# A two-layer trunk on one core: the delta rule's triangular system from raw keys without 48 transposes, weight buffers in memory of their own, last transposes pinned to later matmuls

## Chip, core and metric

The kernel runs on one NeuronCore of a Trainium2 chip. Its time is device microseconds of one execution, from start to end on that core. Time before: 2292.58 us, the median of three runs.

## What is computed

Two layers over 256 tokens with 2048 features, all in float32. Layer 0 mixes the tokens by eight heads of differential attention and eight heads of a gated delta rule. Layer 1 mixes them by sixteen heads of attention in three dilations. Behind each mixer stands an MLP with 8192 hidden features and a squared ReLU. The change touches the delta rule, which the reference states in chunks:

```python
bq = l2_norm(bq); bk = l2_norm(bk)              # keys and queries to length 1
g = -exp(b_a_log) * softplus(ba + b_dt_bias);   beta = sigmoid(bb)
q = q * dk ** -0.5;   gc = cumsum(g)
decay_incl = exp(where(causal, gc[:, None] - gc[None, :], -inf))
kb = k * beta[..., None]
m = (kb @ k.T) * strict(decay_incl)
rhs = concat([v * beta[..., None], kb * exp(gc)[..., None]])
u, w = triangular_solve(eye + m, rhs)           # unit lower triangular
attn = (q @ k.T) * decay_incl
# step over chunks: v_new = u - w @ state;  o = (q*exp(gc)) @ state + attn @ v_new
#                   state = state * exp(g_last) + (k*exp(g_last - gc)).T @ v_new
```

and the frame around it:

```python
x = x + diff_delta_mixer(rms_norm(x, ab_norm), ...)   # w_in 2048 x 7184, w_out 2048 x 2048
x = x + squared_relu_mlp(rms_norm(x, mlp_norm[0]), mlp_w1[0], mlp_w2[0])
x = x + dilated_mixer(rms_norm(x, c_norm), ...)       # w_in 2048 x 6144, w_out 2048 x 2048
x = x + squared_relu_mlp(rms_norm(x, mlp_norm[1]), mlp_w1[1], mlp_w2[1])
```

## The kernel before

**Dense products.** Every product with a weight matrix goes through `dense` (L191). A weight tile of 128 features by 512 columns is loaded by the SP queue (`wload`, L176), split into a high part by a cast on ScalarE (ACT, tile names ending in `h`, L204) and a low part by a subtraction on VectorE (DVE, ending in `l`, L205, recorded at the helper's line L107). Each half of the 256 tokens then takes three matmuls on TensorE (PE): high by high (L210), high by low (L211), low by high (L212). The split weights lie in `wq[0]`, a memory pool of six slots of each part. Casts and subtractions are put 60 places ahead in the order (`high_priority(offset=AHEAD)`).

**Order of the work.** The program is written out flat, and a scheduler fixes each engine's order at compile time from program order, priorities and its own estimate of when inputs are ready. Everything between the dense products is written as generators in three streams, `g` (delta rule), `s` (convolutions, attention, norms) and `o` (outputs). `drip()` in `dense` advances `g` and `s` in turn, one step for each 128 features, so that a step of `g` comes once in two. `flush` advances them all without dense work between. `issue_after(ins)` makes the instructions that are traced inside it come after `ins` on the same engine.

**Layer 0's mixer** (0 to about 450 us, then the output products `wo` to 510.7 us). `do_b` computes q and k of two heads, `do_bv` v, `do_a` and `do_av` the differential attention's, and the gates come with `z2`. `gdn` (L617) works on one pair of heads `s` at a time, four pairs one behind the other (tiles `g0` to `g3`), each with two heads and two chunks of 128 tokens, that is four 128 x 128 tiles. In its steps: `qk` is turned to token-major by transposes on PE (`kp`, `qp`), squared and summed, and the keys `kh` are scaled to length 1. The row `dd` of cumulated gates is read back from DRAM by a DMA and made the decay. `kh` is transposed back (`kt` into `khT`), `pk` is key times key, `m` is `pk` by beta and decay. `m` goes to DRAM and its 16 x 16 diagonal blocks come back (`mb`) to be inverted on DVE; `m` is also transposed (`tt` into `mT`). `pa` is query times key, `am` is that by the decay, and it is transposed as well (second `tt` into `aT`). Then two levels of block elimination (`lp`, `ly`, `lx`), `u` and `w`, the state, and the output.

**Small operations.** `tt`, `stt` and `ts` are DVE's (L107, L113, L117 or L119), `act` is ACT's (L123, L125), `transpose` is PE's (L235). PSUM tiles of the small matmuls come from two pools of two buffers each, `ps_t` for transposes and `ps_m` for products.

**Transitions.** `next_norm` (L295) prepares the next stage's left operand from a finished quarter `n` of `x` (512 features): sums of squares, then transposes to feature-major (`xb`, `xc`, `xd`), split like the weights. The last quarter (`n == 3`) is transposed on PE in the first dense product of the next stage. The stages open memory pools one after the other; what one stage frees, the next takes. Before, `wq0` is the first pool of the first mixer and `wq1`, `wq2` and `wq3` take the same place in the next stages.

Of the kernel before, what the change touches and what calls it, by code (L numbers as in the profile page):

```python
# [19 lines left out]
P = 128  # L20
# [30 lines left out]
def _constants():  # L51
# [36 lines left out]
def trunk(  # L88
# [145 lines left out]
    def transpose(o, i, k=P):  # L234
        E.transpose(o, i, ident[:k, :k])  # L235
# [51 lines left out]
    def turn_quadrant(src, dst, i):  # L287
# [3 lines left out]
        for j in range(4):  # L291
            dv = dst[32 * j:32 * j + 32].rearrange("p c (h t) -> p h c t", h=NH)
            V.transpose(out=dv[:, :, :, q], in_=sv[:, :, :, j, :])  # L293

    def next_norm(n, norm, nm, dst, pool=None):  # L295

        stats_block(xs[n], n, nm + "s")
        if n == 3:
            for _ in range(3):
                yield  # L300
        yield from xt_block(xs[n], n, norm, nm, dst, pool if n < 3 else None)
        if n == 3:
            stats_end(nm + "e")
            yield

    def add_to_x(n, ps):
# [49 lines left out]

    sp.tile([P, 96], F32, tag="fill", name="fill", bufs=1)
    warm = sp.tile([P, 512], F32, tag="junk", name="warm")
# [19 lines left out]
    with ExitStack() as mix:  # L378
        wq[0] = mix.enter_context(tc.tile_pool(name="wq0", bufs=1))
        op = mix.enter_context(tc.tile_pool(name="op", bufs=1))  # L380
# [19 lines left out]
        def behind(gen):  # L400

            while True:
                with tc.issue_after(last_mm[0].ins):
                    if next(gen, gen) is gen:
                        return
                yield

# [93 lines left out]
        beta = mp.tile([P, NH, 8], F32, name="beta")  # L501
        nbeta = mp.tile([P, NH, 8], F32, name="nbeta")
        gg = mp.tile([P, NH, 8], F32, name="gg")
# [7 lines left out]
        def gates(a, b):  # L511
            ts(beta, b, 0.5, 0.5, ALU.mult, ALU.add)
            ts(nbeta, beta, -1.0, None, ALU.mult)
            tt(a, a, dtb.unsqueeze(1).broadcast_to([P, NH, 8]), ALU.add)
# [29 lines left out]
            act(flat(egl), e, AF.Exp)  # L544
            ngc = sp.tile([P, 16], F32, tag="ngc", name="ngc")
            ts(ngc, flat(gc), -1.0, None, ALU.mult)
            yield
            pc = ps_t("pgt")
            transpose(pc[:16, :P], ngc)
            row = sp.tile([P, 512], F32, tag="junk", name="grow_t")[:16, :P]  # L550
# [47 lines left out]
        def v_side(raw, rnm, g, vb, nm):  # L598
            a = mp.tile([P, 4, T], F32, tag="qka", name=nm + "a")
            yield from conv(raw, rnm, [16 + 4 * g + c for c in range(4)], a, nm)  # L600
            for h in range(NH):
                t = ps_t(f"{nm}v{h}")
                for c in range(4):
                    transpose(t[:, c * P:(c + 1) * P], a[:, c, h * P:(h + 1) * P])
                tt(vb[:, h], quads(t), beta[:, h, 4 * g:4 * g + 4].unsqueeze(2).broadcast_to([P, 4, P]), ALU.mult)
            ready.add(f"v{g}")
            yield

        def qk_conv(raw, rnm, s, qks):
# [5 lines left out]
            ready.add(f"qk{s}")  # L615

        def gdn(qks, s, vb, nm):  # L617

# [8 lines left out]
            kh = mt("kh")  # L627
            for w, o, c in (("k", 0, 2), ("q", 4, 0)):
# [6 lines left out]
                if w == "k":  # L635
                    S.copy(kh, quads(pt))
            yield
            rs = mp.tile([P, 8], F32, tag="g_rs", name=nm + "rs")
            rsqrt(rs, ssq, 8, 1.0, nm)
            for i in range(4):  # L640
                ts(kh[:, i, :], kh[:, i, :], rs[:, i:i + 1], None, ALU.mult)
            sq = mp.tile([P, 4], F32, tag="g_sq", name=nm + "sq")
            ts(sq, rs[:, 4:8], 128.0 ** -0.5, None, ALU.mult)

            dd = mt("dd")
            nc.sync.dma_start(
                dd.rearrange("p (h e) c -> p h e c", h=NH),
                bass.AP(scg.tensor, scg.offset + 2 * s * P, [[0, P], [8 * P, NH], [P, 2], [1, P]]))
            for i, (h, e) in enumerate(tiles):
                hd = 2 * s + e  # L650
                stt(dd[:, i, :], dd[:, i, :], gc[:, h, hd:hd + 1], cst("causal"), ALU.add, ALU.min)
            act(dd, dd, AF.Exp)
            for _ in range(3):
                yield
            khT, kd, kbg = mt("khT"), mt("kd", n=2), mt("kbg", n=2)
# [3 lines left out]
            S.copy(khT, quads(t))  # L659
            for e in range(2):  # L660
                hd = 2 * s + e
                ts(kd[:, e, :], kh[:, e, :], egl[:, 0, hd:hd + 1], None, ALU.mult)
                ts(kbg[:, e, :], kh[:, 2 + e, :], egc[:, 1, hd:hd + 1], beta[:, 1, hd:hd + 1], ALU.mult, ALU.mult)
            yield
            m, am = mt("m"), mt("am")
            pk = ps_m(nm + "pk")
            for i, (h, e) in enumerate(tiles):
                E.matmul(pk[:, i * P:(i + 1) * P], lhsT=khT[:, i, :], rhs=khT[:, i, :], start=True, stop=True)
            for i, (h, e) in enumerate(tiles):
                hd = 2 * s + e  # L670
                stt(m[:, i, :], pk[:, i * P:(i + 1) * P], nbeta[:, h, hd:hd + 1], dd[:, i, :], ALU.mult, ALU.mult)

            scr, sxy = scm[s % 2], scx[s % 2]
            nc.sync.dma_start(images(scr), m)
# [3 lines left out]
            mT, aT = mt("mT"), mt("aT")  # L678
# [16 lines left out]
            for j in range(3):  # L695
                n, w = 3 - j, j + 1
                tv = tm[:, :4 * n * w].rearrange("p (b r c) -> p b r c", b=4, r=n)
                xr = part(x0, (j + 1) * BLK, B4, (BLK, n), (1, w))
                tt(tv, part(mb, (j + 1) * BLK + j, B4, (BLK, n), (0, w)), part(x0, j * BLK, B4, (0, n), (1, w)), ALU.mult)
                tt(xr, tv, xr, ALU.add)  # L700
            for b in (4, 8):
                for d in range(0, BLK, 2 * b):
# [3 lines left out]
                    full = [32, b, b, b]  # L706
                    tt(tv, mb[:, lo, hi].unsqueeze(2).broadcast_to(full),
                       x0[:, hi, hi].rearrange("p k c -> p c k").unsqueeze(1).broadcast_to(full), ALU.mult)
# [14 lines left out]
            yield  # L723
            pa = ps_m(nm + "pa")
            for i, (h, e) in enumerate(tiles):
                E.matmul(pa[:, i * P:(i + 1) * P], lhsT=qk[:, e, h * P:(h + 1) * P], rhs=khT[:, i, :], start=True, stop=True)
# [4 lines left out]
            for i in range(4):  # L731
# [31 lines left out]
            while f"v{s // 2}" not in ready:  # L763
                yield
            yield
            u, wT = mt("u", share="m"), mt("wT", n=2, share="khT")
# [435 lines left out]
```

## Time and profile before

| | |
|---|---|
| median of three runs | 2292.58 us (2292.51 to 2294.17) |
| the profiled execution | 2293.58 us; span from first to last instruction 2291.8 us |
| mean granted TensorE clock | 0.999 |
| PE busy | 2279.2 us, 99% of the span, 10536 matmuls |
| PE weight loads | 1887.6 us, 82% |
| DVE busy | 1670.6 us, 73% |
| ACT busy | 1195.0 us, 52% |
| DMA | 420.11 MB read, 185 GB/s over the span |
| first mixer | 0 to 510.7 us |
| first MLP | to 1209.3 us |
| second mixer | to 1589.3 us |
| second MLP | to 2291.8 us |

Matmuls are pipelined, and their recorded durations overlap: a 512-column matmul is recorded with 0.39 us and the next starts 0.23 us after it. What a piece of work costs PE is therefore read from starts, not from durations. A float32 matmul of the small products stands as two records, a transpose as one. An engine's idle time is put down to what released it.

### The profile page before, as it was taken

To read this page: it belongs to the slowest core of one execution; us is meant where nothing else is said; L and a number is where in the kernel's file an instruction comes from. 1 tells how busy PE (TensorE), PEld (TensorE's weight loads), DVE (VectorE), ACT (ScalarE), POOL (GpSimd) and SP (SyncE) were. 2 spreads that over 40 slices of the span, in tenths; PEclk is the share of its full clock that TensorE was granted. 3 is DMA by queue.
4 is the path that set the end of the run, shared out by engine and by line. 5 is a ranking of instruction groups with operands and counts; after the bars stand their busy time and mean duration, and the time that the engine had idled before them with its cause. 6 is when DMAs were issued, how large, how long until landed. Compare 5 with 4: busy or idle time off the path is not lost.

```text
span 2291.8 us, 29876 instructions
## 1 busy us (share of the span) xinstructions
PE 2279.2 (99%) x10536; PEld 1887.6 (82%) x10536; DVE 1670.6 (73%) x3027; ACT 1195.0 (52%) x1865; POOL 5.6 (0%) x15
## 2 busy tenths in 40 slices
PE   9999999999999999999999999999999999999999
PEld 8887888788888888888888888888888888888887
DVE  6868797867757746846888888986775775775774
ACT  6557666655534534534545565555543543543553
POOL 0000000000000000000000000000000000000000
PEclk9999999999999999999999999999999999999999
DMA  8655564456666666666656555555666666666665
GB/s 259 192 172 159 143 182 134 141 177 199 200 194 186 200 194 189 197 195 190 194 192 193 183 176 176 174 184 168 194 194 194 194 194 194 191 195 194 188 208 165
DMA packets 271546, 426.54 MB, mean 186 GB/s; under 512 B 22386, under 2 KB 102436, under 8 KB 271396
## 3 DMA queue, kind: packets, MB, share of 16 engines
q1 hardware_dynamic: 271220, 424.57, 61.3%
q8 instruction: 82, 1.34, 0.3%
q14 instruction: 68, 0.56, 0.1%
q10 hardware_dynamic: 176, 0.07, 0.0%
HBM read 420.11 MB, written 4.46 MB: 185 GB/s over the span
## 4 chain that ended last, share of the span: by engine, by line
PE 94%; DVE 3%; DMA 1%; ACT 1%; issue 1%; SPq 0%; ACTq 0%
PE m_0p L211 3%; PE n_2p L211 3%; PE n_1p L212 3%; PE n_0p L212 3%; PE m_3p L212 3%; PE m_3p L210 3%; PE m_2p L212 3%; PE m_2p L210 3%; PE m_1p L212 3%; PE m_1p L210 3%; PE n_0p L210 3%; PE n_1p L211 3%; PE n_2p L212 3%; PE m_0p L212 3%; PE n_2p L210 3%; PE n_1p L210 3%
## 5 line engine op out<-in xcount | busy, mean ns | idle before, releaser
L107 DVE TENSOR_TENSOR n_3l<-n_3r,n_3h 128x1024 fp32r<-128x1024 f32 x64 | 78.4, 1224 | 76.8 <-ACT n_3h L204 76.7
L107 DVE TENSOR_TENSOR n_2l<-n_2r,n_2h 128x1024 fp32r<-128x1024 f32 x64 | 78.4, 1224 | 76.8 <-ACT n_2h L204 76.7
L107 DVE TENSOR_TENSOR m_0l<-m_0r,m_0h 128x1024 fp32r<-128x1024 f32 x64 | 78.1, 1225 | 73.4 <-ACT m_0h L204 73.0
L107 DVE TENSOR_TENSOR n_1l<-n_1r,n_1h 128x1024 fp32r<-128x1024 f32 x64 | 78.4, 1224 | 67.7 <-ACT n_1h L204 66.9
L204 ACT CAST n_2h<-n_2r 128x1024 fp32r<-128x1024 f32 x64 | 67.5, 1054 | 100.2 <-PE n_2p L212 59.9
L204 ACT CAST n_3h<-n_3r 128x1024 fp32r<-128x1024 f32 x64 | 67.5, 1054 | 100.2 <-PE n_3p L212 59.9
L204 ACT CAST m_0h<-m_0r 128x1024 fp32r<-128x1024 f32 x64 | 67.1, 1054 | 97.2 <-PE m_0p L212 59.9
L204 ACT CAST n_1h<-n_1r 128x1024 fp32r<-128x1024 f32 x64 | 67.5, 1054 | 92.8 <-PE n_1p L212 59.9
L107 DVE TENSOR_TENSOR m_1l<-m_1r,m_1h 128x1024 fp32r<-128x1024 f32 x64 | 78.4, 1225 | 36.9 <-ACT m_1h L204 35.9
L204 ACT CAST m_1h<-m_1r 128x1024 fp32r<-128x1024 f32 x64 | 67.5, 1054 | 66.6 <-PE m_1p L212 38.3
L204 ACT CAST m_3h<-m_3r 128x1024 fp32r<-128x1024 f32 x64 | 67.5, 1054 | 57.3 <-PE m_3p L212 39.9
L204 ACT CAST n_0h<-n_0r 128x1024 fp32r<-128x1024 f32 x64 | 67.5, 1054 | 57.3 <-PE n_0p L212 39.9
L204 ACT CAST m_2h<-m_2r 128x1024 fp32r<-128x1024 f32 x64 | 67.5, 1054 | 57.3 <-PE m_2p L212 39.9
L107 DVE TENSOR_TENSOR n_0l<-n_0r,n_0h 128x1024 fp32r<-128x1024 f32 x64 | 78.4, 1225 | 25.8 <-ACT n_0h L204 24.0
L107 DVE TENSOR_TENSOR m_3l<-m_3r,m_3h 128x1024 fp32r<-128x1024 f32 x64 | 78.4, 1225 | 25.7 <-ACT m_3h L204 23.9
L107 DVE TENSOR_TENSOR m_2l<-m_2r,m_2h 128x1024 fp32r<-128x1024 f32 x64 | 78.4, 1225 | 25.7 <-ACT m_2h L204 23.7
L293 DVE STREAM_TRANSPOSE m_0hT<-m_0r 32x256 f32<-32x256 f32 x128 | 55.8, 436 | 5.8 <-ACT m_0r L123 3.7
L293 DVE STREAM_TRANSPOSE m_1hT<-m_1r 32x256 f32<-32x256 f32 x128 | 55.8, 436 | 5.7 <-ACT m_1r L123 3.6
L293 DVE STREAM_TRANSPOSE m_2hT<-m_2r 32x256 f32<-32x256 f32 x128 | 55.8, 436 | 5.7 <-ACT m_2r L123 3.6
L293 DVE STREAM_TRANSPOSE m_3hT<-m_3r 32x256 f32<-32x256 f32 x128 | 55.8, 436 | 5.7 <-ACT m_3r L123 3.6
L210 PE MATMUL n_0p<-n_0h,m_0hh 128*128 128x512 f32 x64 | 24.9, 389 | 0.0
L211 PE MATMUL n_0p<-n_0l,m_0hh 128*128 128x512 f32 x64 | 24.9, 389 | 0.0
(2553 smaller groups left out, 7388.3 us busy)
## 6 DMA issues: line engine op xcount, KB each, us to landing
m_0r<-in_mlp_w_dram SPq DMA_DIRECT2D x64, 512.0 KB, 4.2
m_1r<-in_mlp_w_dram SPq DMA_DIRECT2D x64, 512.0 KB, 3.8
m_2r<-in_mlp_w_dram SPq DMA_DIRECT2D x64, 512.0 KB, 4.2
m_3r<-in_mlp_w_dram SPq DMA_DIRECT2D x64, 512.0 KB, 3.8
n_0r<-in_mlp_w_dram SPq DMA_DIRECT2D x64, 512.0 KB, 4.2
n_1r<-in_mlp_w_dram SPq DMA_DIRECT2D x64, 512.0 KB, 4.2
n_2r<-in_mlp_w_dram SPq DMA_DIRECT2D x64, 512.0 KB, 4.3
n_3r<-in_mlp_w_dram SPq DMA_DIRECT2D x64, 512.0 KB, 4.3
```

Of the source, the lines that this page charges most:

```text
L107: V.tensor_tensor(out=o, in0=a, in1=b, op=op)
L204: cast[0] = S.copy(whs, w)
L210: E.matmul(o, lhsT=sh, rhs=wh, start=kc == first, stop=False)
L211: E.matmul(o, lhsT=sh, rhs=wl, start=False, stop=False)
L212: last_mm[0] = E.matmul(o, lhsT=sl, rhs=wh, start=False, stop=kc == last)
L293: V.transpose(out=dv[:, :, :, q], in_=sv[:, :, :, j, :])
```

## The change

In `gdn` nothing is scaled to length 1 before the products any more. `pk` and `pa` take the convolved `qk` tiles as they are, which are feature-major already, and the norms go into per-token scalars (`cc`, `nk`, `sq`). Since key times key is symmetric, `mT` is made directly from `pk` with a transposed mask (`causal` is transposed in the constants, and the gate row and column change sign), and `pa` is formed with key as the stationary side, so that `aT` comes out directly. Twelve transposes of each pair of heads go (`kt` and twice `tt`, four tiles each), with three ACT copies from PSUM. `v` is no longer multiplied by beta on DVE but copied by ACT, and scaled in place by ACT before its use. The read of `dd` is issued one step earlier, and `pa` follows `pk` by one step. The weight pool of the first mixer stays open and serves the second mixer too; the MLPs open their pool of activations (`hp0`, `hp1`) first and that of split weights behind it. `next_norm` for `n == 3` waits one step instead of three and pins each part behind the last dense matmul that was traced before it.

```diff
-    put("causal", np.where(low, 0.0, NEG))
+    put("causal", np.where(low, 0.0, NEG).T)
...
+    def behind(gen):
+        while True:
+            with tc.issue_after(last_mm[0].ins):
+                if next(gen, gen) is gen:
+                    return
+            yield
...
         stats_block(xs[n], n, nm + "s")
         if n == 3:
-            for _ in range(3):
-                yield
-        yield from xt_block(xs[n], n, norm, nm, dst, pool if n < 3 else None)
-        if n == 3:
+            yield
+            yield from behind(xt_block(xs[n], n, norm, nm, dst))
             stats_end(nm + "e")
             yield
+        else:
+            yield from xt_block(xs[n], n, norm, nm, dst, pool)
...
+    wq_mix = wq[0] = ctx.enter_context(tc.tile_pool(name="wq0", bufs=1))
     with ExitStack() as mix:
-        wq[0] = mix.enter_context(tc.tile_pool(name="wq0", bufs=1))
...
-                tt(vb[:, h], quads(t), beta[...].broadcast_to([P, 4, P]), ALU.mult)
+                S.copy(vb[:, h], quads(t))
...
+        LEAD, LAND = 3, 6
...
-                    S.copy(kh, quads(pt))
-            yield
...
-            for i in range(4):
-                ts(kh[:, i, :], kh[:, i, :], rs[:, i:i + 1], None, ALU.mult)
+                    S.copy(kh[:, :2], quads(pt[:, :2 * P], 2))
+                    for e in range(2):
+                        ts(kbg[:, e, :], pt[:, (2 + e) * P:(3 + e) * P], egc[...], None, ALU.mult)
             dd = mt("dd")
             nc.sync.dma_start(dd..., scg...)
+            yield
...
+            stt(nk, ssq[:, 0:4], EPS, rs[:, 0:4], ALU.add, ALU.mult)
+            tt(cc[:, 0], rs[:, 0:4], rs[:, 0:4], ALU.mult)
+            tt(cc[:, 0]..., cc[:, 0]..., beta[:, :, 2 * s:2 * s + 2], ALU.mult)
+            ts(cc[:, 1], cc[:, 0], -1.0, None, ALU.mult)
...
-            for _ in range(3):
-                yield
-            t = ps_t(nm + "kt")
-            for i in range(4):
-                transpose(t[:, i * P:(i + 1) * P], kh[:, i, :])
-            S.copy(khT, quads(t))
             for e in range(2):
-                ts(kd[:, e, :], kh[:, e, :], egl[...], None, ALU.mult)
-                ts(kbg[:, e, :], kh[:, 2 + e, :], egc[...], beta[...], ALU.mult, ALU.mult)
-            yield
+                ts(kd[:, e, :], kh[:, e, :], egl[...], cc[:, 0, e:e + 1], ALU.mult, ALU.mult)
+            for _ in range(LEAD):
+                yield
             pk = ps_m(nm + "pk")
-                E.matmul(pk[...], lhsT=khT[:, i, :], rhs=khT[:, i, :], start=True, stop=True)
-                stt(m[:, i, :], pk[...], nbeta[...], dd[:, i, :], ALU.mult, ALU.mult)
+                kt = qk[:, 2 + e, h * P:(h + 1) * P]
+                E.matmul(pk[...], lhsT=kt, rhs=kt, start=True, stop=True)
+                stt(mT[:, i, :], pk[...], cc[:, 1, i:i + 1], dd[:, i, :], ALU.mult, ALU.mult)
...
-            t = ps_t(nm + "tt1")
-                transpose(t[:, i * P:(i + 1) * P], m[:, i, :])
-            S.copy(mT, quads(t))
+            pa = ps_m(nm + "pa")
+                E.matmul(pa[...], lhsT=qk[:, 2 + e, ...], rhs=qk[:, e, ...], start=True, stop=True)
+                stt(aT[:, i, :], pa[...], cc[:, 0, i:i + 1], dd[:, i, :], ALU.mult, ALU.mult)
             yield
...
-            pa = ps_m(nm + "pa")
-                E.matmul(pa[...], lhsT=qk[:, e, ...], rhs=khT[:, i, :], start=True, stop=True)
-            tt(am, quads(pa), dd, ALU.mult)
-            for _ in range(3):
-                yield
-            t = ps_t(nm + "tt2")
-                transpose(t[:, i * P:(i + 1) * P], am[:, i, :])
-            S.copy(aT, quads(t))
-            for _ in range(3):
+            for _ in range(LAND):
                 yield
...
             while f"v{s // 2}" not in ready:
                 yield
+            for i, (h, e) in enumerate(tiles):
+                v = vb[:, h, 2 * (s % 2) + e, :]
+                act(v, v, AF.Identity, scale=nk[:, i:i + 1])
             yield
...
-    with tc.tile_pool(name="wq1", bufs=1) as wq[0], tc.tile_pool(name="hp0", bufs=6) as hp:
+    with tc.tile_pool(name="hp0", bufs=6) as hp, tc.tile_pool(name="wq1", bufs=1) as wq[0]:
         mlp(0, nb, hp, lambda n: streams["s"].append(next_norm(n, 2, f"xc{n}", cb, hp)))
...
-        wq[0] = mix.enter_context(tc.tile_pool(name="wq2", bufs=1))
+        wq[0] = wq_mix
...
-    with tc.tile_pool(name="wq3", bufs=1) as wq[0], tc.tile_pool(name="hp1", bufs=6) as hp:
+    with tc.tile_pool(name="hp1", bufs=6) as hp, tc.tile_pool(name="wq3", bufs=1) as wq[0]:
         mlp(1, nb1, hp, done1)
```

More of the change, by code (lines that the diff above doesn't have):

```diff
@@ L398, in xt_blocks @@
                     yield
[L400 to L405, printed above, removed]
-                yield
         blocks = xt_blocks()
@@ L501, in trunk @@
         beta = mp.tile([P, NH, 8], F32, name="beta")
-        nbeta = mp.tile([P, NH, 8], F32, name="nbeta")
+        ngc = mp.tile([P, 16], F32, name="ngc")
         gg = mp.tile([P, NH, 8], F32, name="gg")
@@ L652, in gdn @@
             act(dd, dd, AF.Exp)
-            for _ in range(3):
+            kd = mt("kd", n=2)
+            for e in range(2):
+                ts(kd[:, e, :], kh[:, e, :], egl[:, 0, 2 * s + e:2 * s + e + 1], cc[:, 0, e:e + 1], ALU.mult, ALU.mult)
+            for _ in range(LEAD):
                 yield
-            khT, kd, kbg = mt("khT"), mt("kd", n=2), mt("kbg", n=2)
-            t = ps_t(nm + "kt")
-            for i in range(4):
-                transpose(t[:, i * P:(i + 1) * P], kh[:, i, :])
@@ L659, in gdn @@
[L659 to L663, printed above, removed]
-            yield
-            m, am = mt("m"), mt("am")
+            mT, aT = mt("mT"), mt("aT")
             pk = ps_m(nm + "pk")
             for i, (h, e) in enumerate(tiles):
-                E.matmul(pk[:, i * P:(i + 1) * P], lhsT=khT[:, i, :], rhs=khT[:, i, :], start=True, stop=True)
@@ L669, in gdn @@
-            for i, (h, e) in enumerate(tiles):
-                hd = 2 * s + e
-                stt(m[:, i, :], pk[:, i * P:(i + 1) * P], nbeta[:, h, hd:hd + 1], dd[:, i, :], ALU.mult, ALU.mult)
+                kt = qk[:, 2 + e, h * P:(h + 1) * P]
+                E.matmul(pk[:, i * P:(i + 1) * P], lhsT=kt, rhs=kt, start=True, stop=True)
+            for i in range(4):
+                stt(mT[:, i, :], pk[:, i * P:(i + 1) * P], cc[:, 1, i:i + 1], dd[:, i, :], ALU.mult, ALU.mult)
             scr, sxy = scm[s % 2], scx[s % 2]
-            nc.sync.dma_start(images(scr), m)
+            nc.sync.dma_start(images(scr), mT)
@@ L764, in gdn @@
                 yield
+            for i, (h, e) in enumerate(tiles):
+                v = vb[:, h, 2 * (s % 2) + e, :]
+                act(v, v, AF.Identity, scale=nk[:, i:i + 1])
             yield
```

37 lines of the change are left out of this document (19 added, 18 removed).

## The prediction

> **What bounds the kernel now.** The page first, for the span and the engines; then busy time by stretches, for the layer 0 mixer where most of the change lies. The columns of the stretches are length, then busy time and count of PE, its weight loads, DVE, ACT and POOL, then granted clock, DMA share and GB/s.
>
> ```profile
> span 2291.8 us, 29876 instructions
> PE 2279.2 (99%) x10536; PEld 1887.6 (82%) x10536; DVE 1670.6 (73%) x3027; ACT 1195.0 (52%) x1865; POOL 5.6 (0%) x15
> 50.00:150.00 100.00, 100.00 (x492) 83.32 (x492) 82.81 (x201) 63.30 (x129) 1.17 (x3) 1.00 0.66 194
> 150.00:250.00 100.00, 98.27 (x509) 80.45 (x508) 73.99 (x209) 61.37 (x148) 0.22 (x2) 1.00 0.52 150
> 250.00:350.00 100.00, 98.76 (x564) 84.17 (x563) 81.20 (x218) 65.70 (x158) 2.02 (x3) 1.00 0.59 170
> 350.00:450.00 100.00, 98.55 (x536) 79.06 (x535) 80.36 (x268) 67.13 (x188) 0.95 (x1) 1.00 0.46 136
> ```
>
> PE bounds it everywhere: 12.6 us of idle in 2291.8, at a clock of 1.00. So only two things can shorten it: less work on PE, or fewer of PE's waits. DVE is busy 74 to 83% in these stretches, near enough to PE that it must be watched. The waits of PE in the mixer, by the view of who waited for whom (50 to 511 us), are all on DVE, 4.1 us together:
>
> ```profile
> PE d1t L235 <- DVE d1qk L107: 1.2, 1, 1.2
> PE d2ot L235 <- DVE d2o L117: 1.1, 1, 1.1
> PE g1lx L235 <- DVE g1xy L107: 0.6, 1, 0.6
> PE d0at L235 <- DVE d0aa L113: 0.5, 1, 0.5
> PE g1kt L235 <- DVE g1kh L117: 0.5, 1, 0.5
> PE g3tt L235 <- DVE g3m L113: 0.2, 1, 0.2
> ```
>
> **Part 1: 48 transposes go.** The price of one group of four is read from starts, in the timeline around one that goes (pair 2's first `tt`), beside the plain dense rhythm of the last output product:
>
> ```profile
> 299.33 0.39 PE L212 MATMUL a1p<-a1h,xa3l 128*128 128x512 f32 x1
> 299.57 0.60 PE L235 MATMUL g2tt<-ca,g2m 128*128 128x128 f32 x4
> ...
> 300.47 0.40 PE L212 MATMUL a1p<-a1h,xa3l 128*128 128x512 f32 x1
> 508.02 0.39 PE L210 MATMUL wo13p<-wo13h,d3oh 128*128 128x512 f32 x1
> ...
> 510.51 0.39 PE L212 MATMUL wo13p<-wo13h,d3ol 128*128 128x512 f32 x1
> ```
>
> From 508.02 to 510.51 lie 11 intervals of matmuls with 512 columns: 2.49 / 11 = 0.226 us each. From 299.33 to 300.47 are 1.14 us, in which start one L212, one L210, one L211 (0.68 us) and the group: 0.46 us for four, 0.115 each. Three groups a pair, four pairs, 12 x 0.46 = 5.5 us of pure PE time. The products `pk` and `pa` stay, in number and shape.
>
> The recorded duration is another number:
>
> ```profile
> L235 PE MATMUL g2kt<-ca,g2kh x4: 270/272/272, 292.7 to 293.0; 128*128 128x128 f32 x4
> ```
>
> The Trainium skill (TensorE: Matmul & The Clock Gate, Part 4: PE-mode transpose) gives about 275 ns for a transpose inside a kernel; the duration of this row agrees. By that price the 48 would be worth 48 x 0.275 = 13.2 us, an estimate from the page. I take the starts, since the four start at 292.7 to 293.0 and each next one does not wait for the end of the last.
>
> Two of the waits above go with their instructions: `g1kt` on the scaled keys and `g3tt` on `m`, 0.7 us. The new `pk` and `pa` need only the convolved tiles, which are done before `gdn` starts, so nothing is late in their place.
>
> **Part 2: what DVE and ACT get instead.**
>
> ```profile
> L117 DVE TENSOR_SCALAR g2kh<-g2kh,g2rs 128x128 f32<-128x128 f32 x4 | 0.9, 282 | 0.0
> L107 DVE TENSOR_TENSOR g2am<-g2pa,g2dd 128x512 f32<-128x512 f32 x1 | 0.7, 672 | 0.0
> L113 DVE SCALAR_TENSOR_TENSOR g2m<-g2pk,nbeta,g2dd 128x128 f32<-128x128 f32 x4 | 1.2, 346 | 0.0
> L113 DVE SCALAR_TENSOR_TENSOR g2dd<-g2dd,gc,ca 128x128 f32<-128x128 f32 x4 | 1.2, 346 | 1.4 <-DMA g2dd<-scg 1.4
> L659 ACT COPY g2khT<-g2kt 128x512 f32<-128x512 f32 x1 | 0.6, 583 | 0.0
> L123 ACT ACTIVATE g0o<-g0po,g0sq 128x128 f32<-128x128 f32 x2 | 0.8, 376 | 0.0
> ```
>
> DVE, for a pair: out go four scalings of `kh` (1.13), `am` (0.67) and half of a group's two products of v by beta (the form of `am`, 0.67), together 2.47 us. In come four products for `aT` (the form of `m`, 1.38) and four operations of 4 columns for `nk` and `cc`, which at no more than the `kh` row are 1.13 at most: 2.51. `kbg` gives one scalar to `kd`, which is even. So DVE is even or a little better. ACT, for a pair: out go the copies `khT`, `mT`, `aT` (1.75) and half the copy of `kh` (0.29); in come one copy of v (0.58) and four scalings of 128 x 128 (4 x 0.376 = 1.50): 2.04 against 2.08, even. I cost both at nothing. What hides them is PE's dense stream: casts are made up to six slots ahead, 6 x 6 x 0.226 = 8.1 us of matmuls. If that cover were gone, the four scalings would delay the casts queued behind them on ACT by 1.5 us a pair, 6.0 us in all.
>
> One edit speaks against the change: `am` was one instruction of 512 columns, `aT` is four of 128, 1.38 against 0.67 us. The Trainium skill (VectorE: DVE Perf Modes, The TRN2 errata) says that a fixed cost is paid per instruction and advises 512 columns or more; these two rows agree. It is inside the sum of DVE above; were those 0.71 us a pair all to become waits of PE, 2.8 us of the gain would be lost.
>
> The read of `dd` moves one step ahead on SP's queue, past one weight load at most; its buffer is free, since the pairs run one behind the other. A step of `g` is two slices of 128 features, 12 x 0.226 = 2.7 us, so the 1.4 us that DVE sat for `dd` is covered. There are 14 steps to `lp` instead of 15, so pair 3 starts some 8 us sooner; I count no gain for it.
>
> **Part 3: the transitions.** The timeline at the end of the first mixer (its last matmul is the row at 510.51 above) and of the first MLP, and the ends of the third:
>
> ```profile
> 510.98 2.95 ACT L204 CAST m_0h<-m_0r 128x1024 fp32r<-128x1024 f32 x3 [4.04 <-PE wo13p L212]
> 511.01 0.44 PE L235 MATMUL xb3t<-ca,xs 128*128 128x128 f32 x2
> 511.69 0.55 PE L235 MATMUL xb3t<-ca,xs 128*128 128x128 f32 x3 [0.24 <-DVE xs L107]
> 512.08 0.74 PE L210 MATMUL m_0p<-m_0h,xb0h 128*128 128x512 f32 x2
> 512.66 0.49 PE L235 MATMUL xb3t<-ca,xs 128*128 128x128 f32 x3
> 513.34 0.50 PE L211 MATMUL m_0p<-m_0l,xb0h 128*128 128x512 f32 x1 [0.19 <-DVE m_0l L107]
> 513.67 0.39 PE L212 MATMUL m_0p<-m_0h,xb0l 128*128 128x512 f32 x1
> 1209.11 0.39 PE L212 MATMUL n_3p<-n_3h,m_3hl 128*128 128x512 f32 x1
> 1209.54 3.74 ACT L204 CAST c0h<-c0r 128x512 fp32r<-128x512 f32 x7 [5.17 <-PE n_3p L212]
> 1209.61 0.44 PE L235 MATMUL xc3t<-ca,xs 128*128 128x128 f32 x2
> 1210.21 0.73 PE L210 MATMUL c0p<-c0h,xc0h 128*128 128x512 f32 x2 [0.17 <-ACT c0h L204]
> 1210.78 0.49 PE L235 MATMUL xc3t<-ca,xs 128*128 128x128 f32 x3
> ...
> 1211.35 0.39 PE L212 MATMUL c0p<-c0h,xc0l 128*128 128x512 f32 x1
> 1589.08 0.39 PE L212 MATMUL co13p<-co13h,e7ol 128*128 128x512 f32 x1
> ...
> 1592.24 0.39 PE L212 MATMUL m_0p<-m_0h,xd0l 128*128 128x512 f32 x1
> ```
>
> The first cast of the next stage's weights waits until the last product of the stage before has read its own, although ACT stands idle for 4.04 and 5.17 us: old and new split weights share memory. PE then lives on transposes and on matmuls that need a high part alone. Loss: from 510.51 to 513.67 are 3.16 us, work in it four dense matmuls (0.90) and eight transposes (0.92), 1.34 lost. From 1209.11 to 1211.35 are 2.24, with four dense (one L211 is left out above) and five transposes, 1.48, so 0.76 lost. The third is 3.16 long like the first, 1.34. Together 3.4 us. With the weights apart, casts can run while the old product still does, PE goes on with dense matmuls, and the transposes, pinned some four slices later, find `xs` ready and are needed only at slice 12. Bounds: 0 (casts still held) and 3.4; I take 3.2, near the upper end, as these rows show no other holder of the casts.
>
> **The sum.** 5.5 + 0.7 + 3.2 = 9.4 us. The profiled execution took 2293.58 us, 1.0 above the median of the runs: 2293.6 - 9.4 = 2284.2, and against the median 2283.2.
>
> **The rivals.**
> - *Swallowed.* PE's freed time before a wait on DVE becomes a longer wait. Pair 0's groups lie where PE is 100.00 busy and are safe; the nine others lie where it waits. All nine lost: 4.1 us, 2287.3. For it: five of the six waits are on DVE work that stays or is only shifted. Against: those four stretches idle at most 1.7 us in 100.
> - *The casts are still held* by some other tile of the closed stage: the 3.2 us stay, 2286.4. With *swallowed* as well: 2290.5, no change.
> - *More waits go.* With pairs earlier and PSUM less crowded, the other 3.4 us of waits go too: 2279.8.
> - *Transposes are worth their recorded duration*, 48 x 0.272 = 13.1 instead of 5.5: 2275.6. Against it stands the starts' reading. This is the price of the Trainium skill's page named above.
> - *Slower: `pk` and `pa` hold PSUM.* They can now run before `dd` exists, and then keep both `ps_m` buffers until DVE multiplies by it; the next small product stands at the head of PE's queue, with the dense stream behind it. The chain of waits has the landing:
>
> ```profile
> 220.06 6.63 DMA g2dd<-scg
> ```
>
> A full landing waited out in each pair is 26.5 us, 2309.7; it makes the kernel slower from 3.5 us a pair on (14.0 us, 2297.2). Against: `pk` comes four steps behind the read, 4 x 2.7 = 10.8 us.
>
> **How the numbers follow.** Forecast 0.56 (2281 to 2285.5), swallowed 0.17, casts held 0.09, both 0.04, more waits gone 0.08, recorded duration 0.02, slower 0.04. 0.2%, about what a measurement of this kernel can tell, is 4.6 us: faster is below 2288.0. A quarter of *swallowed* and a tenth of *held* may end above that: faster 0.87, same 0.09, slower 0.04. The range takes in the neighbours, 2279.0 to 2288.5.
>
> **What would show it.** 48 fewer transposes (L235) on PE. At each transition the first `m_0h` or `c0h` starts before the last matmul of the old stage, and L212 to L212 over the border is 0.23 us. The waits for `g1kt` and `g3tt` are gone. Wrong would be: new waits of PE on `aT` or `mT` or on a PSUM buffer behind `pk`; casts late behind the scalings of `v`; or the waits on `d1qk` and `d2o` grown by what went.

## The result, and the profile after

The changed kernel took 2280.0 us, median of four runs (2278.82 to 2281.64); the kernel before, run beside it, 2292.85 (2292.51 to 2294.17). The ratio is 0.9942, with a 95% interval of 0.9926 to 0.9958, so it is faster by 10 to 17 us. The forecast was 2283.2 with a range of 2279.0 to 2288.5: the time lies inside it, 3.2 us below the forecast. The profiled execution of the changed kernel took 2278.82 us. Among the runs below, one of the kernel before (2514.77 us, at a granted clock of 0.854) and one of `j_dummies` (8203.85) are slow and left out of the ratios, though not of the medians.

The page of the changed kernel begins (busy time, share of the span, instructions of each engine):

```profile
span 2277.0 us, 29780 instructions
PE 2268.2 (100%) x10488; PEld 1883.1 (83%) x10488; DVE 1666.1 (73%) x3034; ACT 1194.0 (52%) x1873; POOL 5.6 (0%) x15
```

There are 48 matmuls fewer on PE, 10536 to 10488 (transposes are counted as matmuls). DVE is 4.5 us shorter than before and ACT 1.0. PE's idle time fell from 12.6 to 8.8 us. What is left of PE's waits between 30 and 500 us, by the view of who waited for whom (total, times, longest):

```profile
PE d0at L235 <- DVE d0aa L113: 0.9, 2, 0.7
PE g3po L794 <- DVE g3u L113: 0.6, 1, 0.6
PE d2at L235 <- DVE d2aa L113: 0.6, 2, 0.4
PE bv1v L235 <- ACT g2j L125: 0.2, 1, 0.2
```

Before, six waits made 4.1 us; now they are 2.3. `g1kt` and `g3tt` are gone with their instructions. `d1t`, `d2ot` and `g1lx`, which wait on work that the change leaves alone, are gone too; `d0at` grew from 0.5 to 0.9, and the other three are new. The stretches of the mixer, in the columns explained with those of before:

```profile
34.00:150.00 116.00, 115.95 (x603) 98.55 (x603) 91.15 (x225) 73.42 (x155) 1.18 (x3) 1.00 0.70 205
150.00:250.00 100.00, 99.07 (x520) 81.99 (x519) 75.35 (x216) 63.73 (x157) 0.22 (x2) 1.00 0.51 152
250.00:350.00 100.00, 99.75 (x568) 85.97 (x567) 81.17 (x232) 66.97 (x167) 2.03 (x3) 1.00 0.59 170
350.00:450.00 100.00, 98.68 (x517) 79.53 (x516) 84.45 (x281) 67.78 (x188) 0.95 (x1) 1.00 0.51 156
```

The third stretch idles 0.25 us where it idled 1.24 before. The two transitions that the prediction showed now look like this in the timeline (start, duration, engine, line, tile; in brackets the idle time before it and what ended it):

```profile
490.19 1.05 ACT L204 CAST m_0h<-m_0r 128x1024 fp32r<-128x1024 f32 x1
...
498.86 1.37 DVE L107 TENSOR_TENSOR xs<-wo13p,xs 128x512 f32<-128x512 f32 x2 [1.49 <-PE wo13p L212]
499.12 0.39 PE L212 MATMUL wo13p<-wo13h,d3ol 128*128 128x512 f32 x1
499.35 0.39 PE L210 MATMUL m_0p<-m_0h,xb0h 128*128 128x512 f32 x1
499.57 0.39 PE L211 MATMUL m_0p<-m_0l,xb0h 128*128 128x512 f32 x1
499.80 0.39 PE L212 MATMUL m_0p<-m_0h,xb0l 128*128 128x512 f32 x1
...
504.79 0.60 PE L235 MATMUL xb3t<-ca,xs 128*128 128x128 f32 x4
...
1194.77 1.15 ACT L204 CAST c0h<-c0r 128x512 fp32r<-128x512 f32 x2 [1.01 <-DMA c0r<-in_c_w_in_dram]
1196.42 0.39 PE L212 MATMUL n_3p<-n_3h,m_3hl 128*128 128x512 f32 x1
1196.65 0.39 PE L210 MATMUL c0p<-c0h,xc0h 128*128 128x512 f32 x1
```

The first cast of `m_0h` starts 8.9 us before the old stage's last matmul instead of 0.5 us behind it, and PE goes from 499.12 to 499.35, its plain rhythm of 0.23 us, over the border. The cast of `c0h` shown waits for its own weights to land, not for a matmul.

**Where the 14.75 us between the two profiled spans come from.** I divide the span by three starts on PE: the last matmul of the first dense product `b0p`, the last of the mixer's last output product `wo13p` (510.51 before, 499.12 after), and those of the stages behind. The first of them, before and after:

```profile
34.13 0.39 PE L212 MATMUL b0p<-b0h,xa3l 128*128 128x512 f32 x1
```

```profile
32.77 0.39 PE L212 MATMUL b0p<-b0h,xa3l 128*128 128x512 f32 x1
```

So the mixer from there on took 476.38 us before and 466.35 after: 10.03 less. The loss at a border is the time from the old stage's last matmul to the new stage's 48th dense matmul, less 48 x 0.2267 us and 0.1133 for each transpose between. It went from 1.37, 0.80 and 1.37 us to 0.08, 0.09 and 0.09: 3.3 less. Another 1.36, the difference of the two rows above, lies in the start-up, and is not the change's (0.1 is left over): PE's first 145 instructions, up to these rows, are the same in the fourteen kernels profiled here, and yet the last one started anywhere from 32.4 to 35.0. All kernels below are therefore compared by their mixer (from the last `b0p` to the last `wo13p`) and their borders; the stretch of the first MLP is the rest of it, from the 48th dense matmul behind its border to its last. Kernels that leave the mixer as it is in the changed one gave 466.45 to 466.88, on two chips, and one that leaves it as before gave 476.33, so such a stretch says about half a microsecond where whole runs say two or three.

### The profile page after: what moved, and what is told of

The parts are those of the page before. It is cut to its first block, busy times and chain, and to the rows that moved or that the text cites. A ratio compares the mean times of both kernels' runs of the same rounds, so it can differ in the third digit from the quotient of the medians.

```text
span 2277.0 us, 29780 instructions
## 1 busy us (share of the span) xinstructions
PE 2268.2 (100%) x10488; PEld 1883.1 (83%) x10488; DVE 1666.1 (73%) x3034; ACT 1194.0 (52%) x1873; POOL 5.6 (0%) x15
## 4 chain that ended last, share of the span: by engine, by line
PE 96%; DVE 3%; ACT 1%; DMA 1%; issue 0%; SPq 0%; DVEq 0%; ACTq 0%
PE m_0p L210 3%; PE m_0p L212 3%; PE m_0p L211 3%; PE n_2p L211 3%; PE n_0p L212 3%; PE m_3p L212 3%; PE m_2p L212 3%; PE n_1p L212 3%; PE m_1p L212 3%; PE m_1p L210 3%; PE n_1p L211 3%; PE n_2p L212 3%; PE n_2p L210 3%; PE n_0p L211 3%; PE n_0p L210 3%; PE m_3p L211 3%
```

## The experiments

### The two halves alone

`a_trans_only` is the kernel before with the memory of the split weights and the pin of the last transposes; `b_gdn_only` is the changed kernel with these undone.

```diff
 # a_trans_only, against before
+    wq_mix = wq[0] = ctx.enter_context(tc.tile_pool(name="wq0", bufs=1))
-    with tc.tile_pool(name="wq1", bufs=1) as wq[0], tc.tile_pool(name="hp0", bufs=6) as hp:
+    with tc.tile_pool(name="hp0", bufs=6) as hp, tc.tile_pool(name="wq1", bufs=1) as wq[0]:
 ...
+            yield from behind(xt_block(xs[n], n, norm, nm, dst))
```

> The kernel before with the transitions of the change alone (weight pools apart, last transposes pinned); the delta rule as before. Theory (each part is worth what the PE starts show): the first mixer ends where it ended before (last matmul of wo13 at 510.5 us, within 0.3 but for the start-up), each of the three borders is 1.30, 0.77 and 1.30 us shorter, together 3.4 us: some 2289.4 us. Rival (the borders only gain because the new mixer leaves ACT and DVE freer before them): less than half of that, 2291 us or more. Rival (moving the pools also helps the mixer): below 2288 us.

> The changed kernel with the transitions put back as before. Theory: from the end of the first dense product (b0p) to the last matmul of wo13 it takes 466.4 us as in the changed kernel, 10.0 less than before, and the three borders are as long as before; some 2283.4 us. Rival (mixer's gain needs the moved pools): over 468 us for that stretch and over 2285 us.

Against before at 2293.8 us, `a_trans_only` took 2290.52 (ratio 0.9986, 0.9976 to 0.9995) and `b_gdn_only` 2282.84 (0.9955, 0.994 to 0.997). In `a_trans_only` the mixer is 476.33 us and the borders lose 0.08, 0.08 and 0.09; in `b_gdn_only` the mixer is 466.59 and the borders 1.38, 0.81 and 1.37. The halves don't touch each other: 0.14% and 0.45% against 0.58% for both.

### The pin without the memory, the memory without the pin

```diff
 # c_no_pin, against the changed kernel
-            yield
-            yield from behind(xt_block(xs[n], n, norm, nm, dst))
 ...
+            for _ in range(3):
+                yield
+        yield from xt_block(xs[n], n, norm, nm, dst, pool if n < 3 else None)
 # d_old_memory, against the changed kernel
-        wq[0] = wq_mix
+        wq[0] = mix.enter_context(tc.tile_pool(name="wq2", bufs=1))
 ... (and the pools of activations and weights in their old order, three places)
```

> The changed kernel with next_norm of before: weight pools apart, the last transposes neither pinned nor earlier. Theory (memory frees the casts, the pin keeps the transposes from standing ahead of ready matmuls): casts of m_0h still start before the last wo13 matmul; transposes that the scheduler puts at once behind it make PE wait for xs (0.27 and 0.41 us were seen before), so each border of the MLPs loses 0.3 to 0.8 us of the 1.30 gained, 1 to 2 us in all. Rival (the pin is worth nothing): borders as in the changed kernel, within 0.1 us each.

> The changed kernel with the weight pools placed as before, transposes pinned. Theory (the memory holds the casts): the first m_0h starts 0.4 us after the last wo13 matmul again; the pinned transposes can't fill that time, so PE stands for cast and subtraction, some 0.4 + 1.05 for the first L210 and 1.24 more for the first L211, 2.3 to 2.7 us a border of an MLP and 1.0 to 1.5 at c0: 2 to 4 us slower than with the transitions of before, some 2286 us. Rival (the pin alone does it): borders within 0.3 us of the changed kernel's.

Each ran once. `c_no_pin` took 2280.44 us; its first border, in the timeline:

```profile
500.77 0.39 PE L212 MATMUL wo13p<-wo13h,d3ol 128*128 128x512 f32 x1
501.00 0.39 PE L210 MATMUL m_0p<-m_0h,xb0h 128*128 128x512 f32 x1
501.22 0.39 PE L211 MATMUL m_0p<-m_0l,xb0h 128*128 128x512 f32 x1
```

It crosses at 0.23 us like the changed kernel. The transposes of the last quarter don't come forward into the border: with the weights ready, the scheduler puts them into the dense product by itself. The first MLP's stretch is 686.43 us against 685.44, and the difference is eight transposes that fall inside it instead of ahead. So the pin is worth nothing within 0.1 us a border, and my expectation of it fell. `d_old_memory` took 2286.83, and its first border shows why the pin needs the memory:

```profile
499.66 0.39 PE L212 MATMUL wo13p<-wo13h,d3ol 128*128 128x512 f32 x1
501.23 0.73 PE L210 MATMUL m_0p<-m_0h,xb0h 128*128 128x512 f32 x2 [1.18 <-ACT m_0h L204]
502.49 0.50 PE L211 MATMUL m_0p<-m_0l,xb0h 128*128 128x512 f32 x1 [0.53 <-DVE m_0l L107]
502.82 0.39 PE L212 MATMUL m_0p<-m_0h,xb0l 128*128 128x512 f32 x1
```

PE stands idle for the casts, and the transposes that filled this time before now come at 507.6. The three borders lose 2.37, 1.37 and 3.99 us, 7.7 together, 4.2 more than with old memory and no pin (`b_gdn_only`); the third alone loses more than the 2.3 to 2.7 that I expected of it. The whole gain of part 3 is the memory's.

### What four transposes cost

In the second products of the first MLP, 48 groups of four transposes of a constant are added, so that none waits for an input.

```diff
 # e_price, in dense(), for 16 products of the first MLP
+            if extra and j in (4, 7, 10):
+                t = ps_t(f"{nm}x{kc}")
+                with tc.issue_after(last_mm[0].ins):
+                    for i in range(4):
+                        transpose(t[:, i * P:(i + 1) * P], cst("ones"))
```

> The changed kernel with 48 more groups of four transposes (of a constant, into a PSUM tile that nobody reads), three in each second product of the first MLP, each pinned behind a dense matmul. There PE has no other waits, so it measures the price of a group. Theory (starts count): 0.45 us a group, 21.8 us more in the first MLP (its span from the first m_0p to the last n_3p 697.1 -> 718.9 us). Rival (a transpose costs its recorded duration, 0.272 us): 52 us more. In the first MLP's second products the DVE and ACT work is unchanged.

One run: 2305.94 us. The first MLP grew from 685.44 to 709.75, 24.31 us, which is 0.506 for a group and 0.127 for a transpose. My expectation by starts was 21.8; by the recorded duration of 0.272 the 192 would have cost 52 us. That rival is out, and with it the 275 ns of the Trainium skill (TensorE: Matmul & The Clock Gate, Part 4: PE-mode transpose) as a price, though not as a duration; the page has that figure for bf16, these transposes are of float32. The timeline around one group shows where 0.506 and the forecast's 0.46 part:

```profile
670.99 0.39 PE L212 MATMUL n_3p<-n_3h,m_1hl 128*128 128x512 f32 x1
671.22 0.60 PE L240 MATMUL n_3x<-ca 128*128 128x128 f32 x4
671.58 0.48 PE L210 MATMUL n_3p<-n_3h,m_2hh 128*128 128x512 f32 x1
671.89 0.40 PE L211 MATMUL n_3p<-n_3l,m_2hh 128*128 128x512 f32 x1
672.13 0.40 PE L212 MATMUL n_3p<-n_3h,m_2hl 128*128 128x512 f32 x1
672.36 0.40 PE L210 MATMUL n_3p<-n_3h,m_2hh 128*128 128x512 f32 x1
672.60 0.39 PE L211 MATMUL n_3p<-n_3l,m_2hh 128*128 128x512 f32 x1
...
673.98 0.39 PE L211 MATMUL n_3p<-n_3l,m_2hh 128*128 128x512 f32 x1
```

From 670.99 to 672.13 are 1.14 us, exactly the window that the prediction read: 0.46 for the group. But the dense matmuls behind that window still start up to 0.24 us apart, and only some ten matmuls later all are back at 0.227. Over the longer window to 673.98, 2.99 us less 11 x 0.2267, the group costs 0.50. For the change's 12 groups that is 12 x 0.506 = 6.1 us, not 5.5. This is an estimate: in the kernel before, nine of the 12 stand in the dense stream like these, and three among other small operations.

### The transposes put back, and their waits

The mixer gained 10.0 us, and the groups account for 6.1. Where do the other 3.9 come from? `j_dummies` is the changed kernel with the 12 groups put back at the places where they were, but with an input that is long ready (`qk`) and an output that nobody reads.

```diff
 # j_dummies, against the changed kernel
+            def again(nm):
+                t = ps_t(nm)
+                for i, (h, e) in enumerate(tiles):
+                    transpose(t[:, i * P:(i + 1) * P], qk[:, 2 + e, h * P:(h + 1) * P])
 ... (called behind pk, ahead of xc, and at the third of the LAND steps)
```

> The changed kernel with 48 transposes put back into the delta rule as bare PE work: three groups of four in each pair, behind pk, before the inversion and in the middle of the wait before lp, of the raw keys, into PSUM tiles that nobody reads. It leaves out nothing. Theory (the gain of 10.0 us in the mixer is 5.4 of PE time and 4.6 of waits): the mixer grows by 5.4 us, 466.4 -> 471.8, some 2285.4 us; what remains of the gain is waits that the shorter chain removed. Rival (PE time was swallowed, the chain alone matters): under 2 us more. Rival (the transposes and their PSUM tiles were themselves the cause of the waits): 8 us or more.

It took 2286.61 us, median of eight runs; against before at 2294.31 the ratio is 0.9966 (0.9955 to 0.9977). The mixer is 474.38, 8.03 more than the changed kernel's: not my 5.4, but the size of the rival, 8 us or more. The groups' own price of 6.1 leaves 1.9 us of delays that came back with the transposes. PE's waits in the mixer (30 to 511 us):

```profile
PE d0at L235 <- DVE d0aa L113: 1.7, 2, 1.1
PE d2at L235 <- DVE d2aa L113: 1.0, 1, 1.0
PE bv1v L235 <- ACT g2j L125: 0.2, 1, 0.2
PE g2ly L748 <- DVE g2P L107: 0.2, 1, 0.2
```

These four sum to 3.1 us where the changed kernel has 2.3, so 0.8 of the 1.9 is in the list; the rest is in delays too short for it. Counted from starts, intervals on PE that are over 0.15 us longer than their kind's rhythm add up to 10.1 us in the mixer before, 8.0 after and 9.9 here. None of the waits in the list is for an input of the added transposes, and none is one of those that went. So what came back is the size, not the same waits. The added transposes also make the pairs later again (the last `g3po` starts at 441.0 us, against 431.0 in the changed kernel), so the 1.9 may be lateness as well as crowding; this run can't part the two. 2.0 us between this kernel (474.38) and the one before (476.38) stay, at the same number of matmuls of each kind. What differs is the copies, the order, the pairs' place in time, and the inputs that came late: two transposes in a row started 0.114 us apart on average before and 0.110 here, which over 220 of them is 0.8 of the 2.0.

### Does running sooner remove the waits?

The chain of pairs is done earlier in the changed kernel: the last product of pair 3 (`g3po`), by the tile's view with the starts of its first and last matmul, before and after:

```profile
L797 PE MATMUL g3po<-g3u,g3aT x8: 275/275/374, 447.9 to 449.0; 128*128 128x128 f32 x8
```

```profile
L794 PE MATMUL g3po<-g3u,g3aT x8: 275/275/377, 429.2 to 431.0; 128*128 128x128 f32 x8
```

That is 18 us, of which 1.4 are the start-up, and for want of other causes I first took it for the cause of the vanished waits. Three kernels move it. `g_lead6` keeps the changed kernel's instructions and makes it late again; `h_before_sooner` and `l_before_lead1` make the kernel before sooner, at two places.

```diff
 # g_lead6, against the changed kernel
-        LEAD, LAND = 3, 6
+        LEAD, LAND = 6, 6
 # h_before_sooner, against before, ahead of and behind the second group of tt
-            for _ in range(3):
+            for _ in range(2):
                 yield
 # l_before_lead1, against before, behind the decay's exponential
-            for _ in range(3):
-                yield
+            yield
```

> The changed kernel with LEAD = 6 instead of 3: each pair's products come three steps later, some 8 us a pair, so that the last pair ends some 25 us later or where it ended before (g3po at 448 us instead of 429). All instructions are the same. Theory (the other waits went because the chain of pairs runs 10 to 20 us ahead, so that the last pair no longer falls into the flush): 2 to 4 us of the mixer's gain are lost, 468.5 to 470.5 us. Rival (they went because PSUM and ACT are less crowded, or by chance of the order): within 1 us of 466.4.

> The kernel before with two waiting steps of the delta rule left out (before and behind the second tt, 3 to 2 each), so that lp comes 13 steps in instead of 15 and the last pair some 16 us sooner; all instructions are those of before. Theory (in the changed kernel some 4 us of PE waits went because the pairs run earlier, so that less of the last pair is left when the dense stream of the inputs ends): mixer 476.4 -> 473.5 us or less. Rival (they went because of the fewer PSUM tiles and copies): within 1 us of 476.4. Rival (waits for data that was not there yet take their place): longer.

> The kernel before with two waiting steps of the delta rule left out ahead of kt (three to one), where they cover no read of the blocks: the read of xy keeps its seven steps. All instructions are those of before; the last pair runs some 16 us sooner. Theory (the 4 us of PE waits that went beside the transposes' own time went because the pairs run sooner): mixer 476.4 -> 471.5 to 473.5 us. Rival (running sooner is worth nothing by itself; the waits went with the instructions that were removed, or by the order that the scheduler came to): 475.5 us or more, or waits of PE for kh and m (g_kt, g_tt) that grow as much.

`g_lead6` (one run, 2288.46 us): the last `g3po` starts at 449.84, and the mixer is 475.50, 9.15 longer, with not one instruction more. I had expected 2 to 4. The first of its waits in the mixer:

```profile
PE d1at L235 <- DVE d1aa L113: 1.4, 1, 1.4
PE g3lx L235 <- DVE g3xy L107: 1.0, 1, 1.0
PE d3at L235 <- DVE d3aa L113: 0.9, 2, 0.6
PE g3lpz L749 <- ACT g3xy L745: 0.7, 1, 0.7
```

Late is dear: the steps of pair 3 (`g3lx`, `g3lpz` and more, 3.2 us in the list) then wait for each other. With its pairs ending as late as in the kernel before, this kernel is only 0.9 us ahead of it, in spite of 48 transposes fewer; its pair 3 starts later, though (the first `g3kp` at 383.0 us, against 376.3 before).

The other way round, sooner brought nothing. `h_before_sooner` (one run, 2295.11 us) starts its last `g3po` at 436.56 and its mixer is 477.29, 0.9 longer; `l_before_lead1` starts it at 434.85, and the mixer is 476.49, the same as before (2293.03 us, ratio 0.9999, 0.9989 to 1.0008). The waits only changed place. The longest of the one, and then of the other:

```profile
PE g2lp L739 <- DMA g2xy<-scx: 3.2, 1, 3.2
PE d2s L918 <- DVE g3am L107: 1.4, 1, 1.4
```

```profile
PE d2t L235 <- DVE d2qk L107: 1.1, 1, 1.1
PE g2kt L235 <- DVE g2kh L117: 0.9, 1, 0.9
PE bv1v L235 <- ACT g2khT L658: 0.8, 1, 0.8
```

So the forecast of my theory, 471.5 to 473.5 us, fell. But neither kernel is a clean test, for both take their steps from in front of something that then waits. In the first the read of `g2xy` is no longer covered (3.2 us), and without that wait its mixer would be some 2 us shorter than before (an estimate: 477.29 less 3.2, against 476.38). In the second the transposes `kt` wait for `kh` (1.5 us in three pairs) and `bv1v` for the buffer of `kt` (0.8). Waits of this second kind are for what the changed kernel doesn't have. `i_lead1` below makes the changed kernel's pairs another 18 us sooner with no wait at the place where the steps were taken, and it gained nothing either. What the place of the pairs is worth by itself in the kernel before stays open.

### DVE's four small products, and the distance to `dd`

`f_dve_twice` issues the four products for `aT` twice. `i_lead1` takes `pk` two steps closer to the read of `dd` than the changed kernel has it, which is the place where the prediction's rival of a slower kernel would show. `k_diff_step` gives the wait that is now longest, `d0at` on `d0aa`, one step more.

```diff
 # f_dve_twice
                 stt(aT[:, i, :], pa[:, i * P:(i + 1) * P], cc[:, 0, i:i + 1], dd[:, i, :], ALU.mult, ALU.mult)
+                stt(aT[:, i, :], pa[:, i * P:(i + 1) * P], cc[:, 0, i:i + 1], dd[:, i, :], ALU.mult, ALU.mult)
 # i_lead1
-        LEAD, LAND = 3, 6
+        LEAD, LAND = 1, 6
 # k_diff_step, in diff, behind the products for aa
                 yield
+                yield
                 t = ps_t(f"{nm}at{e}")
```

> The changed kernel with each of the four products for aT done twice on DVE, 4 x 0.346 us more a pair, 5.5 us more DVE work in the mixer. Theory (DVE's small changes are hidden by the dense stream): mixer 466.4 us, at most 1.5 more. Rival (DVE work in the delta rule becomes PE waits one for one): 5 us more.

> The changed kernel with LEAD = 1 instead of 3: pk comes two steps behind the read of dd, some 5.4 us, less than the 6.6 us that its landing took once. Theory A (the rival of the prediction: pk and pa then hold both PSUM buffers until dd is there, and PE stands): waits of 1 us or more in each pair on the small products behind pk, mixer 467.5 us or more. Theory B (the chain's earlier end counts for more): g3po some 16 us earlier than 431 us and the mixer 464 to 466 us.

> The changed kernel with one more step in the differential attention between the combination aa on DVE and its transposes, the largest of PE's waits that are left (d0at 0.9 us and d2at 0.6 us by the waits of PE). Theory: those two waits go, mixer 466.4 -> 464.5 to 465.5 us, a gain of 1 to 2 us that three rounds can hardly tell. Rival (the attention of the last pair ends later and holds up the output products): 467 us or more.

`f_dve_twice` (one run, 2278.79 us): 16 products more on DVE, 5.5 us by the 0.342 us that one of them takes, and the mixer is 465.92, no longer than the changed kernel's. DVE's time is free here by that much. No run adds work to ACT.

`i_lead1` (one run, 2281.97 us): the mixer is 467.35, 1.0 longer, for waits on `g2P` (1.3 us) and `d2qk` (1.0). None stands behind `pk`, and the last `g3po` starts at 412.8 us. I had expected 467.5 or more with waits behind `pk`, or 464 to 466 by the earlier end; it is neither. The tiles' view of `dd` and `pk` in this kernel, for pair 0 (the read's issue, the exponential that finishes `dd`, the products) and for pair 2 (the read's issue, the products, their reader on DVE):

```profile
L644 SPq DMA_DIRECT2D g0dd<-scg x1: 367/367/367, 83.3 to 83.3; - x1
L123 ACT ACTIVATE g0dd<-g0dd x1: 643/643/643, 92.6 to 92.6; 128x512 f32<-128x512 f32 x1
L672 PE MATMUL g0pk<-qk x8: 271/275/276, 95.5 to 96.3; 128*128 128x128 f32 x8
L644 SPq DMA_DIRECT2D g2dd<-scg x1: 367/367/367, 184.9 to 184.9; - x1
L672 PE MATMUL g2pk<-qk x8: 273/275/276, 262.9 to 263.6; 128*128 128x128 f32 x8
L113 DVE SCALAR_TENSOR_TENSOR g2mT<-g2pk,g2cc,g2dd x4: 346/346/347, 267.9 to 268.7; 128x128 f32<-128x128 f32 x4
```

In pair 2 `pk` comes 78 us behind the read even here, in pairs 1 and 3 74 and 82. It does hold its buffer for 4 us until DVE takes it, and nobody waits for that. Pair 0 is the near one: `pk` comes 12.2 us behind the read and 2.3 us after `dd` is done. In the changed kernel these are 17.2 and 7.7 us. So the rival's condition was not met in any pair, but in pair 0 of this kernel it was only 2.3 us off.

`k_diff_step` took 2279.02 us (2277.72 to 2279.33; ratio to before 0.9938, 0.9922 to 0.9955). Its mixer is 465.13, 1.2 less than the changed kernel's, and `d0at` fell to 0.2 us, while `d2at`, which got the same step and was to go too, grew from 0.6 to 0.9. By whole runs the two can't be told apart.

## Why the prediction was right, and where it was off

The direction and the kind of each gain were right. The sum was 3.2 us short by the medians; by the stretches the mixer gained 3.8 us more than forecast (10.0 against 6.2) and the borders 0.1.

- **The bound.** "Less work on PE, or fewer of PE's waits": both came. DVE and ACT were costed at nothing. For DVE a run shows it: 5.5 us of more work cost none. For ACT only the profile speaks: it is busy 1.0 us less, and in the mixer's list PE waits for no cast.
- **The price of a group.** 0.46 us was read in a window of three matmuls behind it. The dense matmuls behind that window still come late by up to 0.01 us each, and the whole price is 0.506. That term was 5.5 and measured 6.1.
- **The waits.** This is the step that failed. "Two of the waits above go with their instructions", priced at 0.7 us, was all; measured are 3.9 us of delays, 10.03 less 6.1. Only 1.8 of it can be seen in the list of waits (4.1 to 2.3), because the list leaves out the many short ones. Of the rival *more waits go* (3.4 us above the forecast's 0.7, 2279.8 us) the size is about right, 3.2 more; its reason, "pairs earlier and PSUM less crowded", is not shown. Pairs made earlier without taking anything out gained nothing in three kernels, of which two lost slack elsewhere, and PSUM was not tried by itself. 1.9 of the 3.9 come back when bare transposes are put back, with their buffers and their delay of the pairs. That the other 2.0 belong to copies and inputs that went is only argued.
- **"Pair 3 starts some 8 us sooner".** It started 17 us sooner (`g3kp` at 359.1 instead of 376.3) and ended 18 us sooner, 1.4 of both from the start-up; why twice the forecast is not shown. "I count no gain for it" is not settled either: making the changed kernel late costs 9 us, and making either kernel sooner gained nothing.
- **Swallowed.** PE's freed time did not turn into longer waits. That is settled by the mixer alone: the rival would have left 2287.3 us.
- **Transitions.** 3.2 of 3.4 was taken, and 3.3 measured. That there was "no other holder of the casts" held. The prediction gave the memory and the pin one sum; the memory has all of it, and the pin without the memory costs 4.2 us.
- **`pk` and `pa` hold PSUM.** The distance of 10.8 us, counted in steps, was too short: in the changed kernel 17.2 us lie between the read and the product in pair 0 and 80 to 89 in the others. No wait came behind `pk`, and pair 0 was the one to watch.
- **The start-up.** The sum was made against one profiled execution and compared with another; 1.36 us of the 14.75 between the two spans are the start-up's, and no step of the prediction is about them.

## What to carry to other kernels

Price a small instruction in a dense stream by the starts around it, and in a window long enough for the rhythm to come back; a recorded duration gave twice the cost, and a window of three matmuls nine tenths of it. When instructions are taken out of a chain that the bounding engine waits in, ask for each wait in the list whether its input or its buffer goes, and keep the whole of the waits as an upper end: here 3.9 us went with them. Before you move a chain earlier, look at what its waiting steps cover: three such kernels gained nothing, and in two of them something that the steps had covered waited instead. At a border between stages look at what ends the first cast's wait: if it is the old stage's last matmul, see whether the two share memory; here separate memory repaired it, while a pin alone made it worse.

## What the runs showed of the hardware

In `e_price`, four transposes of 128 x 128 in a stream of matmuls of 512 columns slow the stream behind them: some of the next ten start 0.23 to 0.24 us apart instead of 0.227, and the group costs 0.506 us where the window of three shows 0.46.

The first 33 us differed by up to 2.6 us over fourteen kernels, one profiled execution of each, with the same 145 instructions on PE. The granted clock of the first 34 us was 0.95 before and 1.00 after, by the windows' view:

```profile
0.00:34.00 34.00, 30.92 (x144) 25.37 (x145) 21.35 (x58) 23.40 (x57) 1.20 (x6) 0.95 0.80 256
```

```profile
0.00:34.00 34.00, 31.44 (x154) 26.00 (x155) 22.63 (x71) 23.95 (x59) 1.20 (x6) 1.00 0.81 264
```

The Trainium skill (TensorE: Matmul & The Clock Gate, Part 1, What's actually happening) calls the ramp at the start run-variable, since the window that sets the clock runs freely. These two rows fit that, though they are of two kernels; but `k_diff_step` was granted 1.00 as well and started its last `b0p` at 34.32, so the clock is not all of it.
